# RWKV's chunk chain: both heads of a pair in one full-array matmul, and new durations in the builder's clock

## The chip, the cores and the metric

The kernel runs on one core of one Trainium2 chip. The metric is device time in microseconds (us), from the first to the last instruction of the program plus what lies around it; the median of three runs counts. PE is the matrix engine (TensorE), PEld its weight loads, DVE VectorE, ACT ScalarE, POOL GpSimd, SP the engine that issues nearly all transfers.

## What is computed

One layer of a streaming encoder, for 512 prompt tokens of one stream and 16 tokens each of 8 running streams (640 rows together), model width 1024. The reference, cut:

```python
h = _rmsnorm(x, norm_g)
proj = jnp.einsum('btd,dc->btc', h, w_in)             # 1024 x 10368
o_a = _sb_attend(q, k, v, ...)                        # 16 heads x 64, stick-breaking attention
y_a = jnp.einsum('btc,cd->btd', o_a * jax.nn.silu(z_a), w_o_a)
...
def step(S, inp):                                     # RWKV-7, 16 heads x 64, per token
    sa = jnp.einsum('bhvk,bhk->bhv', S, -kk_t)
    S = (S * w_t[:, :, None, :] + sa[..., None] * (kk_t * a_t)[:, :, None, :]
         + v_t[..., None] * k_t[:, :, None, :])
    return S, jnp.einsum('bhvk,bhk->bhv', S, r_t)
...
y = jnp.einsum('btd,de->bte', g_a * y_a + g_b * y_b, w_out)
return x + y, ...                                     # then a last rmsnorm
```

## The kernel before

**Projections.** The 81 column blocks of `w_in` (128 columns each) and the 8 blocks each of `w_o_b` and `w_o_a` are jobs of `gemm_range`. A job makes two halves of 320 or 322 rows; a half is 8 chunks of three matmuls (high by high, high by low, low by high part of fp32, tile `ps_g`), so a job is 48 matmuls. At the end `oblock` multiplies with `w_out` (tiles `ohi`, `olo`, `mgh`, `mgl`). Matmuls into `ps_g` are called projections below.

**RWKV in pairs of heads.** Heads 2p and 2p+1 lie on partitions 0-63 and 64-127. For a pair, `prep` makes from the projected rows the tiles `H`, `BK` and `AB` for ten chunks (eight of 64 prompt tokens, two with the running streams), `prep2` inverts a triangular matrix per chunk (blocks of 16 on POOL in `INV`, transposed by DVE through `STG`, then joined to 32 and 64 by small matmuls), `samp` brings in the running streams' states, and `chain` goes through the chunks in eight steps. A step first forms `RH` (matmul of `H` with `X` into `ps_b`) and the first part of the output (into `ps_c`); ACT copies `RH` out; then it forms u (`AB` with `RH`); ACT copies u into `X`; then the new state (`BKt` with `X`) and the second part of the output (`AB` with `X`); DVE writes the state to `X`, and the next step may begin. Chunks 8 and 9 (the running streams) go along in step 0, which therefore has three chunks per matmul kind. Each product stands twice, once per head, 64 columns each: `H` by `X` and `BKt` by `X` use 128 rows and 64 columns of the array, `AB` by `RH` or `X` use 64 rows and 64 columns. Every fp32 product is two instructions on PE, which is why the trace counts twice what the program has. `sstate` and `post` finish the states and the output of a pair.

**Attention in pairs of heads** (`aprep`, `attn`) starts when the last pair's `post` is through: scores (`ks` with `qh`, `ql`), two sigmoids on ACT, a running product on DVE (a scan over `kp`), a product into `bt`, transposes of `bt` on PE, a copy to `wt`, and `wt` times the values into `ps_c`. After attention the `w_o_a` jobs follow, whose operand `oAh`, `oAl` is read back through DRAM and split by POOL and DVE (`reload`).

**What sets the order.** The program is written out by a builder. `Clock` keeps an estimate of when each engine is free and each tile ready, from a table of durations in `_Eng.call`; `Driver.run` lets the streams (`prep`, `chain`, `attn` and so on, by priority) issue when their operands are ready by that estimate, and else issues a few more projections (two chunks, six matmuls, at a time) from the main program. The result is one fixed order per engine. A transpose on DVE and a scan are costed there like any other DVE operation; nothing is costed for a change of the array's shape. `calm` and the flags (`chain`, `schain`, `prep`, `amat`) gate the streams.

In `prep`, L777 waits for `chain` and `schain` of pair p-3 before `H` and `AB` are taken (three buffers each); the waits for pair p-2 stand behind the products with `H` and `BK`, ahead of `X`.

Of the kernel before, what the change touches and what calls it, by code (L numbers as in the profile page):

```python
# [26 lines left out]
F32 = mybir.dt.float32  # L27
# [8 lines left out]
D = 1024  # L36
# [52 lines left out]
class Clock:  # L89
# [5 lines left out]
    def __init__(self):  # L95
# [8 lines left out]
        self.near = dict(pe=0.25, act=0.2, dve=0.2, pool=0.15, dma=0.0)  # L104
# [99 lines left out]
class _Eng:  # L204
# [3 lines left out]
    def __getattr__(self, op):  # L208
        f = getattr(self.obj, op)

        def call(*a, **k):
# [7 lines left out]
            if e == "pe":  # L219
                w = k.get("lhsT")  # L220
                if w is None:
                    d = 0.115
                else:
                    m = _cols(w)
                    if w.dtype == F32R:
                        d = max(n / 2360.0, 0.107)
                    elif w.dtype == F32:
                        d = max(0.026 + n * 0.00087, 0.082 if m > 32 else 0.041) if m <= 64 else 0.005 + n / 600.0
                    else:
                        d = 0.06  # L230
            elif e == "act":
                d = 0.05 + n * 0.00086 + 0.1 * sum(hasattr(k.get(x), "tensor") for x in ("scale", "bias"))
# [6 lines left out]
            elif e == "dve":  # L239
                d = 0.066 + n * 0.00105  # L240
                if "scalar" in op:
                    d += 0.03 * sum(hasattr(x, "tensor") and _cols(x) == 1 for x in list(a) + list(k.values()))
                if op == "reciprocal":
                    d = 0.05 + n * 0.0064
            elif e == "pool":
                d = 0.15 + n * (0.0021 if op == "tensor_tensor" else 0.001)
                if op == "tensor_copy":
                    d = 0.2 + n * 0.0035
# [72 lines left out]
def body(tc, ins, outs, dbg=None):  # L321
# [224 lines left out]
    def start():  # L546
        x34 = pers.tile([128, 2, D], F32, tag="H", name="x34", bufs=3)
        srow = pers.tile([88, 3, 128], F32, tag="AB", name="srow", bufs=3)
# [159 lines left out]
    def prep(p):  # L708
# [68 lines left out]
        if p > 2:  # L777
            yield flag("chain", p - 3)
            yield flag("schain", p - 3)
        H = o["H"] = pers.tile([128, 2, 10, 128], F32, tag="H", name="H", bufs=3)  # L780
        AB = o["AB"] = pers.tile([128, 10, 128], F32, tag="AB", name="AB", bufs=3)
        BK = tr.tile([128, 10, 2, 64], F32, tag="BK", name="BK")
        c8 = dict(c=8)
        for h in range(2):
            rs = RS[h]
            stt(H[rs, h, 0:8, 0:64], kkn[rs, 0:512].rearrange("p (c t) -> p c t", **c8), -1.0,
                e1p[rs, :, 0:64], ALU.mult, ALU.mult)
            stt(H[rs, h, 8:10, 0:64].rearrange("p g (b t) -> p g b t", b=4),
# [34 lines left out]
        if p > 1:  # L823
            yield flag("chain", p - 2)
            yield flag("schain", p - 2)
# [931 lines left out]
```

## Time and profile before

| | |
|---|---|
| median of 3 runs | 1248.35 us (1247.88 to 1251.11) |
| profiled execution, its own time | 1252.26 us |
| its span, first to last instruction | 1250.4 us |
| mean granted clock of TensorE | 0.968 |
| busy: PE, DVE, ACT, POOL | 1157.7, 770.0, 626.3, 405.9 us |

The profile shows one execution. Matmuls overlap in the array, so the busy time of a group of them counts overlaps, and what one costs is read from the distance between starts in the timeline. "DVE X" behind an idle time names the engine and the tile that ended it. A granted clock of 1.00 is 2.4 GHz, 0.50 is 1.2 GHz.

### The profile page before, as it was taken

Reading aid. Unit: us, or ns where it says so; the run is one execution under the profiler, and the core shown is the slowest. Engines: PE = TensorE matmul, PEld = TensorE weight load, DVE = VectorE, ACT = ScalarE, POOL = GpSimd, SP = SyncE. Lnnn points to the kernel's source line nnn. Section 1 sums busy time; section 2 is a strip of 40 time slices with the busy share of each in tenths; the row PEclk is TensorE's granted clock in tenths of the full one; section 3 lists DMA queues with packets and bytes.
Section 4 is the critical chain, followed back from the end, with each engine's and each line's share of the span. In section 5 each row is a group of like instructions: output and inputs, shape, how many; then the busy total and the mean of one; then the engine's idle time right before and its main releaser. Section 6 shows DMA issues by size and latency. Waiting matters only on the chain.

```text
span 1250.4 us, 26994 instructions
## 1 busy us (share of the span) xinstructions
PE 1157.7 (93%) x10818; PEld 1033.7 (83%) x10818; DVE 770.0 (62%) x1501; ACT 626.3 (50%) x1328; POOL 405.9 (32%) x603
## 2 busy tenths in 40 slices
PE   7999899999899999999999999998898887999997
PEld 5989778888788798787787788997777776899997
DVE  5575855776856756756756742337777778654334
ACT  5637267466366474474474463534555453413223
POOL 1034341332432350351352241124444446312302
PEclk9999899999999998898999889999999997999999
DMA  5232131322212232311322322395765565246322
GB/s 193 67 107 62 54 104 47 84 88 83 72 58 77 73 85 65 88 55 58 90 58 70 84 79 80 105 255 155 204 177 143 140 177 158 88 131 185 102 100 84
DMA packets 205300, 130.79 MB, mean 105 GB/s; under 512 B 78332, under 2 KB 184696, under 8 KB 205176
## 3 DMA queue, kind: packets, MB, share of 16 engines
q1 hardware_dynamic: 204888, 129.03, 35.5%
q8 instruction: 85, 1.39, 0.5%
q14 instruction: 39, 0.32, 0.1%
q0 software_dynamic: 288, 0.05, 0.0%
HBM read 97.70 MB, written 31.35 MB: 103 GB/s over the span
## 4 chain that ended last, share of the span: by engine, by line
PE 60%; DVE 18%; ACT 11%; issue 5%; POOL 3%; DMA 2%; SPq 0%; DVEq 0%; ACTq 0%; POOLq 0%
PE ps_g L212 42%; PE ps_a L212 9%; PE ps_b L212 6%; DVE kp L212 4%; PE ps_c L212 3%; ACT STG L212 2%; DVE bt L212 2%; ACT AB L212 2%; DVE BK L212 2%; DVE H L212 1%; DVE wlo L212 1%; ACT L212 1%; DVE STG L212 1%; DVE Oa L212 1%; ACT X L212 1%
## 5 line engine op out<-in xcount | busy, mean ns | idle before, releaser
L212 PE MATMUL ps_g<-xh,whi 128*128 128x320 f32 (+1 forms) x1424 | 481.6, 338 | 0.2 <-ACT xh L212 0.2
L212 PE MATMUL ps_g<-xl,whi 128*128 128x320 f32 (+1 forms) x1424 | 448.0, 315 | 5.5 <-DVE xl L212 5.5
L212 PE MATMUL ps_g<-xh,wlo 128*128 128x320 f32 (+1 forms) x1424 | 447.5, 314 | 1.9 <-DVE wlo L212 1.9
L212 PEld LDWEIGHTS ps_g<-xh,whi 128*128 128x128 f32 x1424 | 274.1, 193 | 20.5 <-issue 5.9
L212 PEld LDWEIGHTS ps_g<-xl,whi 128*128 128x128 f32 x1424 | 274.7, 193 | 9.3 <-DVE xl L212 6.5
L212 PEld LDWEIGHTS ps_g<-xh,wlo 128*128 128x128 f32 x1424 | 274.2, 193 | 2.4 <-DVE wlo L212 2.4
L212 DVE TENSOR_TENSOR wlo<-raw,whi 128x1024 fp32r<-128x1024 f32 x97 | 123.5, 1273 | 37.5 <-ACT whi L212 36.5
L212 ACT ACTIVATE whi<-raw 128x1024 fp32r<-128x1024 f32 x97 | 102.6, 1057 | 69.7 <-PE ps_g L212 39.4
L212 POOL TENSOR_TENSOR itmp<-INV 128x28 f32<-128x28 f32 (+6 forms) x112 | 44.7, 399 | 186.5 <-DVE INV L212 178.4
L212 DVE TENSOR_TENSOR_SCAN kp<-kp,amsk 128x256 f32<-128x256 f32 (+3 forms) x80 | 77.2, 973 | 42.3 <-ACT kp L212 42.2
L212 POOL TENSOR_TENSOR bt<-bt,amsk 128x128 f32<-128x128 f32 x64 | 46.9, 738 | 140.8 <-ACT bt L212 75.6
L212 ACT ACTIVATE RH<-ps_b 128x64 f32<-128x64 f32 (+1 forms) x64 | 15.1, 236 | 119.2 <-PE ps_b L212 119.1
L212 ACT ACTIVATE kp<-ps_a 128x512 f32<-128x512 f32 (+3 forms) x72 | 33.0, 459 | 72.7 <-PE ps_a L212 47.1
L212 ACT ACTIVATE sp<-ps_g 128x320 f32<-128x320 f32 x80 | 35.0, 438 | 68.0 <-PE ps_g L212 50.9
L212 ACT ACT_TABLE_LOAD x44 | 56.5, 1283 | 20.7 <-DVE BK L212 13.5
L212 PE MATMUL ps_b<-cst,bt 128*128 128x128 f32 x192 | 34.9, 288 | 24.9 <-DVE bt L212 22.9
L212 POOL TENSOR_TENSOR ux<-X,cst 128x256 f32<-128x256 f32 x32 | 24.3, 781 | 80.2 <-PE ps_b L212 45.0
L212 DVE SCALAR_TENSOR_TENSOR X<-ps_b,wc,SW 64x64 f32<-64x64 f32 x96 | 27.0, 282 | 37.5 <-PE ps_b L212 35.8
L212 PEld LDWEIGHTS ps_b<-cst,bt 128*128 128x128 f32 x192 | 22.3, 144 | 33.1 <-issue 9.7
L212 DVE TENSOR_TENSOR bt<-bt,kp 128x511 f32<-128x511 f32 (+4 forms) x72 | 43.2, 599 | 8.8 <-POOL bt L212 2.0
L212 POOL TENSOR_TENSOR INV<-INV,itmp 128x28 f32<-128x28 f32 (+6 forms) x112 | 44.8, 400 | 8.8
L212 PE MATMUL ps_g<-olo,mgh 128*128 128x256 f32 x160 | 45.0, 281 | 0.0
(250 smaller groups left out, 2299.9 us busy)
## 6 DMA issues: line engine op xcount, KB each, us to landing
raw<-in_w_in_dram SPq DMA_DIRECT2D x81, 512.0 KB
q<-dr_q SPq DMA_DIRECT2D x32, 160.0 KB
Kr<-in_cache_sb_k_dram SPq DMA_DIRECT2D x16, 256.0 KB
Vp<-in_cache_sb_v_dram SPq DMA_DIRECT2D x16, 256.0 KB
raw<-in_w_o_b_dram SPq DMA_DIRECT2D x8, 512.0 KB
raw<-in_w_o_a_dram SPq DMA_DIRECT2D x8, 512.0 KB
oraw<-in_w_out_dram SPq DMA_DIRECT2D x4, 1024.0 KB
dr_zB<-zm SPq DMA_DIRECT2D x8, 320.0 KB
```

What stands on the lines that cost most here:

```text
L212: r = f(*a, **k)
```

## The change

`step` in `chain` multiplies both heads at once: the stationary operand holds both heads' 64 columns, the moving one both heads' 64 columns of `X`, and the result is 128x128, of which only the two diagonal blocks are used afterwards (`heads`). So that u and the output stay separate, `AB` becomes block-diagonal: two fixed tiles `ABD` of 128x10x2x128, whose off-diagonal blocks are set to zero once, by POOL, and which pairs use in turn. `H` changes its layout to put both heads side by side, and has two buffers instead of three. Therefore `prep` waits for `chain` and `schain` of pair p-2 already ahead of `H`. The output tile holds four chunks, so the eight steps are cut into groups of 2, 4 and 2 (before: 4 and 4). The second part of the change is the clock's table: other durations for nearly every kind of operation, and a cost where the array changes its shape.

```diff
-        self.near = dict(pe=0.25, act=0.2, dve=0.2, pool=0.15, dma=0.0)
+        self.near = dict(pe=0.25, act=0.15, dve=0.14, pool=0.15, dma=0.0)
+        self.mode = None
...
+                mode = "full" if r > 64 and m > 64 else (r > 32, r > 64, m > 32, m > 64)
+                if mode != self.clk.mode:
+                    d += 0.1 if self.clk.mode == "full" else 0.2
+                    self.clk.mode = mode
             elif e == "act":
-                d = 0.05 + n * 0.00086 + 0.1 * sum(hasattr(k.get(x), "tensor") for x in ("scale", "bias"))
+                d = 0.065 + n * 0.00085 + 0.1 * sum(hasattr(k.get(x), "tensor") for x in ("scale", "bias"))
+                if out.shape[0] < 64:
+                    d = 0.12 + n * 0.0021
+                elif out.shape[0] < 128:
+                    d += 0.115
...
-                d = 0.066 + n * 0.00105
...
+                d = 0.075 + n * 0.00106
+                if op == "scalar_tensor_tensor":
+                    d = 0.13 + n * 0.00112
...
+                elif op == "tensor_tensor_scan":
+                    d = 0.03 + n * 0.0025
...
+                elif op == "transpose" and len(ins[0].shape) > 2 and ins[0].ap[-1][0] > 1:
+                    d = 2.03
...
-        if p > 2:
-            yield flag("chain", p - 3)
-            yield flag("schain", p - 3)
-        H = o["H"] = pers.tile([128, 2, 10, 128], F32, tag="H", name="H", bufs=3)
-        AB = o["AB"] = pers.tile([128, 10, 128], F32, tag="AB", name="AB", bufs=3)
+        if p > 1:
+            yield flag("chain", p - 2)
+            yield flag("schain", p - 2)
+        H = o["H"] = pers.tile([128, 10, 2, 2, 64], F32, tag="H", name="H")
+        AB = o["AB"] = ABD[p % 2]
...
             for k, c in enumerate(js):
-                for h in range(2):
-                    mm(rh[RS[h], k], lhsT=H[:, h, c, 0:64], rhs=X[:, c, h, :], start=True, stop=True)
-            RH = ch.tile([128, 3, 64], F32, tag="RH", name="RH")
-            act(out=RH[:, 0:n], in_=rh[:, 0:n], func=AF.Copy)
+                mm(pv[:, k], lhsT=H[:, c, 0].rearrange("p h t -> p (h t)"), rhs=xs[c], start=True, stop=True)
+            RH = ch.tile([128, 3, 128], F32, tag="RH", name="RH")
+            act(out=RH[:, 0:n], in_=pv[:, 0:n], func=AF.Copy)
...
             for k, c in enumerate(js):
-                for h in range(2):
-                    rs = RS[h]
-                    mm(u[rs, k], lhsT=AB[rs, c, 0:64], rhs=RH[rs, k], start=True, stop=True)
+                mm(u[k], lhsT=AB[:, c, 0], rhs=RH[:, k], start=True, stop=True)
...
-            for h in range(2):
-                mm(ps[RS[h], 384:448], lhsT=BKt[:, j, h * 64:(h + 1) * 64], rhs=X[:, j, h, :],
-                   start=True, stop=True)
+            mm(pv[:, 2], lhsT=BKt[:, j, :], rhs=xs[j], start=True, stop=True)
...
-        for steps in (((0, 8, 9), (1,), (2,), (3,)), ((4,), (5,), (6,), (7,))):
+        for steps in (((0, 8, 9), (1,)), ((2,), (3,), (4,), (5,)), ((6,), (7,))):
...
+        ABD = [pers1.tile([128, 10, 2, 128], F32, name=f"AB{i}") for i in range(2)]
...
+        for t in ABD:
+            G.memset(t, 0.0)
```

How the order moves, at two places. The first is PE in the chain of the second pair. Before, the end of a step (`BKt` and `AB` with `X`) and the start of the next one (`H` with `X`), with products of the next pair's `prep` (`H` with `BK`) between them:

```order
L212 MATMUL ps_b<-X,BKt 64x64 x2
L212 MATMUL ps_c<-X,AB 64x64 x2
L212 MATMUL ps_a<-H,BK 128x128 x8
L212 MATMUL ps_b<-X,H 64x64 x2
L212 MATMUL ps_c<-X,H 64x64 x2
```

With the change, the last step of that chain, with two sums of squares of `prep` (`nrm`) between its parts:

```order
L213 MATMUL ps_b<-X,H 128x128
L213 MATMUL ps_c<-X,H 128x128
L213 MATMUL ps_a<-nrm,cst 128x320
L213 MATMUL ps_b<-RH,AB_103 128x128
L213 MATMUL ps_a<-nrm,cst 128x320
L213 MATMUL ps_b<-X,BKt 128x128
L213 MATMUL ps_c<-X,AB_103 128x128
```

Each pair of 64-column products became one of 128 columns. Counted over the stretch up to the first attention matmul, PE goes from one array shape to another 536 times before and 140 times with the change; the chain has 768 products before and 384 now.

The second place is PE in the attention of the second pair, between the transposes of the first block of `bt` and those of the next. Before:

```order
L212 MATMUL ps_g<-xh,wlo 128x320
L212 MATMUL ps_b<-cst,bt 128x128 x4
L212 MATMUL ps_a<-ks,qh 128x384
L212 MATMUL ps_a<-ks,ql 128x384
L212 MATMUL ps_b<-cst,bt 128x128 x4
L212 MATMUL ps_g<-xh,whi 128x320
```

With the change, at the same place of the same pair (the first of four such triples of projections is shown):

```order
L213 MATMUL ps_b<-cst,bt 128x128 x4
L213 MATMUL ps_a<-ks,qh 128x384
L213 MATMUL ps_a<-ks,ql 128x384
L213 MATMUL ps_g<-xh,whi 128x320
L213 MATMUL ps_g<-xl,whi 128x320
L213 MATMUL ps_g<-xh,wlo 128x320
```

Twelve projections now stand ahead of the second block's transposes. Counted from the first scores of one pair to those of the next, there are 558 projections in seven pairs before (3399 to 3957 of 5163) and 606 with the change (3573 to 4179). The last attention matmul stands behind projection 4011 before and 4239 with the change; the `w_o_a` jobs begin with projection 4300 in both.

## Rows read from the trace of the kernel before

**Rows 1.** The page: busy time, share of the span and instructions.

```profile
PE 1157.7 (93%) x10818; PEld 1033.7 (83%) x10818; DVE 770.0 (62%) x1501; ACT 626.3 (50%) x1328; POOL 405.9 (32%) x603
```

**Rows 2.** The page: chain that ended last, shares of the span by engine.

```profile
PE 60%; DVE 18%; ACT 11%; issue 5%; POOL 3%; DMA 2%; SPq 0%; DVEq 0%; ACTq 0%; POOLq 0%
```

**Rows 3.** Windows: stretch, length, busy us (instructions) per engine, PEclk, DMA, GB/s.

```profile
27.00:826.00 799.00, 754.84 (x7593) 669.17 (x7593) 498.00 (x1081) 439.67 (x920) 247.96 (x412) 0.96 0.27 78
826.00:1090.00 264.00, 231.15 (x2009) 200.67 (x2008) 184.32 (x241) 128.41 (x300) 116.22 (x137) 0.97 0.59 160
1090.00:1128.00 38.00, 38.00 (x261) 38.00 (x260) 19.78 (x25) 5.31 (x5) 5.26 (x4) 1.00 0.53 169
570.00:575.00 5.00, 5.00 (x92) 4.57 (x85) 1.74 (x5) 0.54 (x2) 0.00 (x0) 0.50 0.03 7
```

**Rows 4.** Timeline of PE, parts of a single-chunk step: start, us, operation, shapes, count.

```profile
402.27 0.31 PE L212 MATMUL ps_g<-xh,wlo 128*128 128x320 f32 x1
402.51 0.34 PE L212 MATMUL ps_b<-X,H 128*64 128x64 f32 x4
402.67 0.29 PE L212 MATMUL ps_c<-X,H 128*64 128x64 f32 x4
...
403.14 0.31 PE L212 MATMUL ps_g<-xl,whi 128*128 128x320 f32 x1
...
403.72 0.31 PE L212 MATMUL ps_g<-xh,wlo 128*128 128x320 f32 x1
403.96 0.33 PE L212 MATMUL ps_b<-RH,AB 64*64 64x64 f32 x4
...
404.48 0.31 PE L212 MATMUL ps_g<-xl,whi 128*128 128x320 f32 x1
```

**Rows 5.** Timeline of PE, the end of a later step.

```profile
410.75 0.31 PE L212 MATMUL ps_g<-xh,wlo 128*128 128x320 f32 x1
410.99 0.34 PE L212 MATMUL ps_b<-X,BKt 128*64 128x64 f32 x4
411.25 0.33 PE L212 MATMUL ps_c<-X,AB 64*64 64x64 f32 x4
...
411.77 0.31 PE L212 MATMUL ps_g<-xl,whi 128*128 128x320 f32 x1
```

**Rows 6.** Timeline of PE, three chunks of u in step 0.

```profile
397.33 0.56 PE L212 MATMUL ps_b<-RH,AB 64*64 64x64 f32 x12
...
398.08 0.31 PE L212 MATMUL ps_g<-xl,whi 128*128 128x320 f32 x1
```

**Rows 7.** Timeline of PE, two full-array fp32 products of 320 columns.

```profile
49.79 1.24 PE L212 MATMUL ps_a<-nrm,cst 128*128 128x320 f32 x4
...
51.01 0.31 PE L212 MATMUL ps_g<-xl,whi 128*128 128x322 f32 x1
```

**Rows 8.** Waits: who waited for whom, us in total, times, longest.

```profile
PE ps_b L212 <- DVE bt L212: 22.9, 28, 2.0
PE ps_b L212 <- DVE X L212: 12.3, 7, 2.6
PE ps_a L212 <- DVE STG L212: 11.5, 7, 2.6
```

**Rows 9.** Timeline of PE around a stall of the inversion.

```profile
565.66 1.05 PE L212 MATMUL ps_a<-STG,AB 16*32 16x16 f32 x64 [2.63 <-DVE STG L212]
...
568.69 0.47 PE L212 MATMUL ps_g<-xh,whi 128*128 128x322 f32 x1
568.95 0.47 PE L212 MATMUL ps_g<-xl,whi 128*128 128x322 f32 x1
```

**Rows 10.** Groups by line and form: shapes, count, busy, mean ns, idle before.

```profile
L212 DVE STREAM_TRANSPOSE STG<-INV 128x1024 f32<-128x1024 f32 x16 | 25.7, 1606 | 13.6 <-POOL INV L212 8.8 <-ACT AB L212 4.4
L212 DVE TENSOR_TENSOR_SCAN kp<-kp,amsk 128x512 f32<-128x512 f32 x16 | 24.3, 1520 | 0.0
L212 POOL TENSOR_SCALAR oAh<-rl 128x640 fp32r<-128x640 f32 x8 | 8.1, 1032 | 8.1 <-DMA rl<-dr_oA 4.6 <-PE ps_c L212 3.4
```

More of the change, by code (lines that the diff above doesn't have):

```diff
@@ L239, in call @@
             elif e == "dve":
[L240 to L244 removed]
+                d = 0.075 + n * 0.00106
+                if op == "scalar_tensor_tensor":
+                    d = 0.13 + n * 0.00112
+                elif op == "tensor_scalar":
+                    d = 0.1 + n * 0.0011 + 0.03 * sum(hasattr(x, "tensor") and _cols(x) == 1
+                                                     for x in list(a) + list(k.values()))
+                elif op == "tensor_tensor_scan":
+                    d = 0.03 + n * 0.0025
+                elif op == "reciprocal":
+                    d = 0.05 + n * 0.0064
+                elif op == "bn_stats":
+                    d = 0.126
+                elif op == "transpose" and len(ins[0].shape) > 2 and ins[0].ap[-1][0] > 1:
+                    d = 2.03
+                if out.shape[0] < 128 and any(_name(x).startswith("ps_") for x in ins if hasattr(x, "tensor")):
+                    d += 0.09
             elif e == "pool":
[L246 removed]
+                d = 0.2 + n * (0.0022 if op == "tensor_tensor" else 0.0012)
                 if op == "tensor_copy":
[L248 removed]
+                    d = 0.15 + n * 0.0035
             else:
@@ L863, in prep2 @@
         o = rw[p]
-        AB = o["AB"]
+        AB = [o["AB"][:, :, 0, 64 * (q // 2):64 * (q // 2) + 64] for q in range(4)]
+        ABt = o["AB"]
         for q in range(4):
@@ L868, in prep2 @@
             i = q % 2
[L869 removed]
+            act(out=STG[rq, :, 0:10], in_=AB[q][rq, :, 32 * i:32 * i + 32].rearrange("p u t -> p t u"), func=AF.Copy)
         yield [STG]
@@ L1049, in step @@
                 if j == 0:
-                    V.tensor_scalar_mul(out=dst, in0=ps[rs, 384:448], scalar1=wc[rs, 0:1])
+                    V.tensor_scalar_mul(out=dst, in0=heads(pv[:, 2], rs), scalar1=wc[rs, 0:1])
                 else:
-                    stt(dst, ps[rs, 384:448], wc[rs, j:j + 1], SW[rs], ALU.mult, ALU.add)
+                    stt(dst, heads(pv[:, 2], rs), wc[rs, j:j + 1], SW[rs], ALU.mult, ALU.add)
             give(ps)
             yield [X]
-        for steps in (((0, 8, 9), (1,), (2,), (3,)), ((4,), (5,), (6,), (7,))):
+        for steps in (((0, 8, 9), (1,)), ((2,), (3,), (4,), (5,)), ((6,), (7,))):
             pob = yield from take("c")
-            pov = pob[:, 0:384].rearrange("p (c v) -> p c v", c=6)
+            pov = pob.rearrange("p (c v) -> p c v", c=4)
             at0 = steps[0][0]
             for js in steps:
-                yield from step(js, [pov[:, c - at0 if c < 8 else c - 4] for c in js])
+                yield from step(js, [pov[:, c - at0 if c < 8 else c - 6] for c in js])
                 if len(js) > 1:
                     drv.spawn(sstate(p), 1)
-            act(out=Oa[:, at0:at0 + 4, :], in_=pov[:, 0:4], func=AF.Copy)
-            done = list(range(at0, at0 + 4))
+            m = len(steps)
+            for h in range(2):
+                act(out=Oa[RS[h], at0:at0 + m, :], in_=heads(pov[:, 0:m], RS[h]), func=AF.Copy)
+            done = list(range(at0, at0 + m))
             if at0 == 0:
-                act(out=Oa[:, 8:10, :], in_=pov[:, 4:6], func=AF.Copy)
+                for h in range(2):
+                    V.tensor_copy(Oa[RS[h], 8:10, :], heads(pov[:, 2:4], RS[h]))
                 done += [8, 9]
```

94 lines of the change are left out of this document (45 added, 49 removed).

## The prediction

> **What bounds the kernel now.** I read the page first: PE is busy for 1157.7 of 1250.4 us [rows 1], and 60% of the chain that ended last runs over PE, no other engine coming near [rows 2]. Then the windows by stage. From 27 to 826 us (projections with RWKV) PE is busy for 754.84 of 799 us, from 826 to 1090 (projections with attention) for 231.15 of 264, and from 1090 to 1128, where only projections are left, for all of 38 us, 261 matmuls, which is 0.1456 us each [rows 3]. So PE sets the time nearly everywhere: whatever stream has nothing ready is covered by projections, and a shorter chain is worth something only as PE time. PE can win in three ways: less work, less idle time (799 - 754.84 = 44 us in RWKV, 264 - 231.15 = 33 us in attention [rows 3]), or less time at half clock (mean granted clock 0.96 and 0.97 there [rows 3]; at 0.5 while gated, that is some 64 and 16 us at 1.2 GHz).
>
> What a burst of chain work costs is seen best in the timeline, from the projection before it to the second projection behind it, less two projections. A lone first part (`H` with `X`, four products): 403.14 - 402.27 - 0.29 = 0.58 us. A lone u: 404.48 - 403.72 - 0.29 = 0.47 [rows 4]. A lone last part: 411.77 - 410.75 - 0.29 = 0.73 [rows 5]. Together 1.78 us for a step with one chunk.
>
> How much of it is products, and how much the change of the array's shape? In the first part, the second pair of products starts 0.16 us behind the first [rows 4], 0.08 each. u with three chunks takes 398.08 - 397.33 = 0.75 us from its start [rows 6], with one 404.48 - 403.96 = 0.52 [rows 4]: four further products of 64 rows add 0.23, 0.058 each. That leaves 0.26, 0.35 and 0.73 - 0.16 - 0.12 = 0.45 us in the three bursts for seven changes of shape, about 0.15 each.
>
> The new products have a neighbour in the trace: two full-array fp32 products of 320 columns take 51.01 - 49.79 - 0.147 = 1.07 us up to the projection that follows [rows 7], 0.535 each, and nothing is lost on going from projections to them or back. For 128 columns that scales to 0.215 us.
>
> **The change part by part.**
>
> *Products.* Of 768 old ones, 448 use 128 rows (0.08) and 320 use 64 rows (0.058): 35.8 + 18.6 = 54 us. The 384 new ones take 384 x 0.215 = 83 us. That is +28 us. The array now multiplies blocks that nobody reads. For one pair of products [rows 4, 6, 7]: 2 x 0.058 = 0.116 against 0.215. The Trainium skill (TensorEngine Tiling (Array Packing), Theoretical Speedup) gives up to 2x for products with at most 64 rows or columns, which speaks against filling the array; with its factor for all products the old ones would cost 41 us and this line would be +41, an estimate.
>
> *Shape changes.* 536 before, 140 now, by the order: 396 fewer x 0.15 = -59 us. With the products, -31. As a check, the 56 steps of one chunk cost 1.78 if alone, now 5 x 0.215 = 1.08, and 56 x 0.70 = 39 us; but many bursts adjoin other small products, whose shape change remains. With 0.13 per change it is -23. I take **-30**, between -23 and -39.
>
> *The clock's table, RWKV.* The order changes where PE waits. The waits named are 11.5 us for `STG` in seven stalls and 12.3 us for `X` in seven [rows 8]. `STG` is transposed on DVE in 1.6 us on average [rows 10], which the old table put at 0.066 + 1024 x 0.00105 = 1.14; the new one has 2.03 for the strided half, so I let these 11.5 us go. `X` waits in DVE's queue behind operations that run beside POOL, whose stretching no table has: I let 4.5 of these and the smaller waits go. **-16** of 44, bounds 0 (the order fits no better) and -26.
>
> *The clock's table, attention.* PE waits 22.9 us for `bt` in 28 stalls [rows 8]. A scan of 512 takes 1.52 us [rows 10]; the old table said 0.066 + 0.54 = 0.60, the new one 1.31. The order shows the cure: 606 projections in place of 558 over seven pairs, 48 x 0.1456 = 7 us, of which twelve stand just ahead of the second block. The projections were there anyway, so the idle time they fill is gained. With the last pair and better places, **-9** of 33, bounds 0 and -18.
>
> *Half clock.* Behind the 2.63 us wait for `STG`, projections stand 0.26 us apart in place of 0.147 [rows 9], and the window from 570 to 575 shows 0.50 [rows 3]: one such stall costs some 9 us x 0.45 = 4 us more than itself. Seven at that price would be 28; the others are shorter, and I take a third, **-9**, bounds 0 and -20.
>
> *What the chain's latency does.* `RH` is twice as wide on ACT, and outputs are copied by halves of the partitions. These are latencies of a stream that waits for its turn anyway, covered by six to twelve projections; 0 for PE. If that cover is gone, PE waits inside the step, which is the bound of the first rival. Two buffers of `H`: pair p now waits for the chain of p-2 one stage earlier, ahead of `H` instead of ahead of `X`. That moves work in the order, and PE is filled with projections meanwhile: 0. Zeroing `ABD` is two POOL operations at the start, ahead of any use of `AB`: 0.
>
> *The end of attention.* This is what becomes late next. With PE time taken from RWKV and attention and projections put in, only 4300 - 4239 = 61 projections (9 us) stand between attention and the `w_o_a` jobs, before 289 (42 us). In these 9 us the last output goes through DRAM and back, and POOL copies eight parts to `oAh` at 1.03 us each [rows 10], 8.3 us in a row, DVE following with `oAl`. A job wants a part every 3 x 0.147 = 0.44 us, so the eighth is due 9 + 3 = 12 us behind attention's last matmul, and it comes at about 1 + 8.3 + 2. I take **+3**, bounds 0 and +10. SP issues the weights for the next jobs behind the store of that output; their 512 KB are due another job later.
>
> *Sum.* -30 - 16 - 9 - 9 + 3 = -61 us against the profiled execution's own 1252.3: 1191.3. That execution lay 3.9 us above the median, so **1187 us** as a median, 4.9% faster.
>
> **The rivals.**
>
> *The stalls stay.* The new table is fitted to means, while DVE beside POOL varies, and four of eight pairs now have the products for `H` and `BK` right beside the `X` copies of step 0. Then only the PE work and the short end count: -30 + 3, 1221 us. For it: 12.3 us of waits for `X` that no entry explains. Against: the `STG` and scan entries were off by 0.5 and 0.9 us, and these are corrected.
>
> *The edges stay: slower.* If the array paid the shape change also between fp32 full-array products and projections (a drain of the pipeline rather than the shape), each of the three bursts of 64 steps would keep both edges: 64 x 3 x 2 x 0.15 = 58 us of the 59 gained come back, and +28 of products remain, 1248 + 28 - 1 = 1275 us with the stalls as they are. It decides from the point where an edge costs 0.08 us. Against it stands the pair of sums of squares, which shows no edge [rows 7].
>
> *Attention ends too late.* If RWKV's longer stretch of the order (its chain ends behind projection 3309, before 3105) makes the end wait in earnest, PE stands for the whole read-back at each of the first `w_o_a` jobs, for 15 to 30 us, and the clock falls too: about 1208 us. For it: the cover fell from 42 to 9 us. Against: the parts come at nearly the pace at which they are wanted.
>
> *More than I take.* All named waits go, and the half clock with them: -39 - 26 - 18 - 20 = -103, 1145 us. It needs every bound at its best.
>
> **How the numbers follow.** Forecast 0.62 (1165 to 1210), the stalls stay 0.18, a late end 0.09, more than I take 0.06, the edges stay 0.05. About 0.3% (3.7 us) is what a measurement of this kernel can tell from no change. Faster: all but the edges and a strip of the stalls' case in which the order makes new waits of 25 us: 0.92. Same 0.03, slower 0.05. The range goes from the forecast's lower end, 1165, to just beyond the case in which the stalls stay, 1223; outside lie the edges, most of "more than I take" and some of the two other cases, about 0.2.
>
> **What the profile after should show.** In the chain, `ps_b<-X,H` with 160 instructions of 128x128 in place of 320, 0.43 us from one part's start to the next projection, and the first projection behind it at the usual distance (if it comes 0.1 later, the edges stay). PE busy in the RWKV stretch lower by some 30 us at the same number of projections. The wait of PE for `STG` near 0, that for `bt` under 15, that for `X` still near 10. Mean clock at 0.975 or more. Projections into `ps_g` from `oAh` soon behind attention, with a few us of waits for `oAl` or `oAh`. Wrong would be: PE idle in RWKV above 40 us again, idle of more than 10 us at the first `w_o_a` job, or a burst that costs as much as before.

## The result, and the profile after

The changed kernel takes 1211.51 us (1208.81 to 1212.96), the kernel before beside it 1249.73 us (1247.88 to 1251.49): a ratio of 0.9692, 95% interval 0.9665 to 0.9719. The forecast was 1187 us in a range of 1165 to 1223: the time lies in the range, 24 us above the forecast and just outside the 1165 to 1210 us that the forecast was given for itself. Of 61 us that were forecast against the profiled execution, 39.3 came (1252.26 to 1212.96). So the question is where the other 22 went, and whether the 39 came from where they were forecast.

The page of the changed kernel: busy time, share of the span (1211.2 us) and instructions.

```profile
PE 1127.9 (93%) x10050; PEld 1053.9 (87%) x10050; DVE 774.2 (64%) x1517; ACT 628.5 (52%) x1344; POOL 403.6 (33%) x605
```

PE's share is the 93% of before [rows 1]: PE works less and waits as before. Its windows, columns as in [rows 3]:

```profile
27.00:826.00 799.00, 749.35 (x6963) 710.31 (x6962) 507.85 (x1099) 447.03 (x947) 246.99 (x408) 0.97 0.27 80
826.00:1090.00 264.00, 246.78 (x2148) 219.22 (x2148) 196.90 (x266) 130.53 (x297) 114.48 (x143) 0.99 0.64 176
```

RWKV's stretch is idle for 799 - 749.35 = 50 us, more than the 44 of before; attention's for 17 in place of 33. (The stretches hold slightly other work, since the program runs ahead.) Most of the rise in RWKV is ahead of projections: they wait 5.3 us there for DVE's `wlo` and `V`, 1.9 before. By the idle times in PE's timeline, between projections, that is ahead of every product that is not one, it is 41.5 us before and 43.1 now (27 to 800 us), and 27.4 and 14.5 (800 to 1090 us); with the waits ahead of projections 43.4 and 49.1, and 32.2 and 16.5. The waits in RWKV, 27 to 826 us (us in total, times, longest), the three largest:

```profile
PE ps_b L213 <- POOL sn L213: 15.5, 6, 5.1
PE ps_b L213 <- DVE X L213: 12.2, 6, 3.9
PE ps_a L213 <- DVE BK L213: 7.1, 4, 2.9
```

`STG` (11.5 us before [rows 8]) is gone, as forecast. In its place stand `sn` and `BK`, which were 0.3 and 1.5 us before, and `X` is as it was. In attention (800 to 1090 us) the wait for `bt` fell from 22.9 us in 28 stalls [rows 8] to

```profile
PE ps_b L213 <- DVE bt L213: 14.0, 17, 1.4
```

The chain's parts, where they stand alone, cost what was forecast. PE's timeline, a lone u and a lone last part:

```profile
169.00 0.31 PE L213 MATMUL ps_g<-xh,wlo 128*128 128x320 f32 x1
169.15 0.38 PE L213 MATMUL ps_b<-RH,AB 128*128 128x128 f32 x2
169.29 0.40 PE L213 MATMUL ps_g<-xh,whi 128*128 128x320 f32 x1
169.52 0.31 PE L213 MATMUL ps_g<-xl,whi 128*128 128x320 f32 x1
...
176.14 0.30 PE L213 MATMUL ps_g<-xh,wlo 128*128 128x320 f32 x1
176.29 0.38 PE L213 MATMUL ps_b<-X,BKt 128*128 128x128 f32 x2
176.50 0.39 PE L213 MATMUL ps_c<-X,AB 128*128 128x128 f32 x2
176.65 0.39 PE L213 MATMUL ps_g<-xh,whi 128*128 128x320 f32 x1
176.88 0.31 PE L213 MATMUL ps_g<-xl,whi 128*128 128x320 f32 x1
```

From the projection before to the second one behind, less two projections: 169.52 - 169.00 - 0.29 = 0.23 us (0.47 before [rows 4]), 176.88 - 176.14 - 0.29 = 0.45 (0.73 before [rows 5]), and a first part likewise 0.45 (0.58). A step is 1.12 us in place of 1.78; the forecast had 1.08. The block products start at a projection's distance (0.15 us), so there is no edge, and the rival in which the edges stay is out.

Summed over RWKV (27 to 800 us), what lies between projections took 304.9 us before and 278.6 after; without the idle time in it, 263.4 and 235.6: 28 us less. That reads like the forecast's -30 for the products. The experiments say otherwise.

### The profile page after: what moved, and what is told of

It is laid out like the page before. It is cut to its first block, busy times and chain, and to the rows that moved or that the text cites. A ratio compares the mean times of both kernels' runs of the same rounds, so it can differ in the third digit from the quotient of the medians.

```text
span 1211.2 us, 25425 instructions
## 1 busy us (share of the span) xinstructions
PE 1127.9 (93%) x10050; PEld 1053.9 (87%) x10050; DVE 774.2 (64%) x1517; ACT 628.5 (52%) x1344; POOL 403.6 (33%) x605
## 5 line engine op out<-in xcount | busy, mean ns | idle before, releaser
L213 PE MATMUL ps_g<-xh,whi 128*128 128x320 f32 (+1 forms) x1424 | 472.7, 332 | 2.5 <-DVE V L213 2.0
L213 DVE TENSOR_TENSOR_SCAN kp<-kp,amsk 128x256 f32<-128x256 f32 (+3 forms) x80 | 74.6, 941 | 31.4 <-ACT kp L213 31.3
L213 ACT ACTIVATE RH<-ps_b 128x128 f32<-128x128 f32 (+1 forms) x64 | 19.4, 303 | 105.7 <-PE ps_b L213 105.5
L213 POOL TENSOR_TENSOR on<-on,V 128x640 f32<-128x640 f32 x8 | 13.6, 1697 | 168.2 <-ACT on L213 168.2
L213 ACT ACTIVATE kp<-ps_a 128x512 f32<-128x512 f32 (+3 forms) x72 | 33.1, 459 | 68.4 <-PE ps_a L213 43.1
L213 DVE SCALAR_TENSOR_TENSOR X<-ps_b,wc,SW 64x64 f32<-64x64 f32 x96 | 27.1, 283 | 42.8 <-PE ps_b L213 41.7
L213 DVE TENSOR_TENSOR bt<-bt,kp 128x511 f32<-128x511 f32 (+4 forms) x72 | 46.8, 650 | 8.4 <-POOL bt L213 0.9
L213 DVE TENSOR_TENSOR AB<-ps_a,cst 64x512 f32<-64x512 f32 (+1 forms) x48 | 28.6, 596 | 32.1 <-PE ps_a L213 32.0
```

The lines of the kernel that those rows point to most:

```text
L213: r = f(*a, **k)
```

## The experiments

The theory after the first look: the products gave the 28 us; the new durations gave 13 us in attention, but in RWKV they made new waits where they took old ones away. The rivals: the waits for `sn` and `BK` come with the chain's change (its products, its two buffers of `H`), or single orders scatter by chance. One suspect needs no run: with the waits for p-2 ahead of `H` and two buffers of `H` put into the kernel before, the builder writes the same order on PE, DVE, ACT and POOL with the new durations, so buffers and flags don't move anything.

All runs; idle is PE's between projections, from its timeline (27 to 800 and 800 to 1090 us; waits ahead of a projection are not in it), clock the mean granted one, cover the projections between attention and the `w_o_a` jobs by the order:

| kernel | median us | ratio (95%) | idle RWKV | idle attn | clock | cover |
|---|---|---|---|---|---|---|
| before | 1250-1252 | 1 | 41.5 | 27.4 | 0.968 | 288 |
| changed | 1211.5 | 0.9692 (0.9665-0.9719) | 43.1 | 14.5 | 0.971 | 60 |
| products_only | 1265.7 | 1.0128 (1.0095-1.0160) | 60.4 | 29.5 | 0.957 | 324 |
| table_only | 1213.5 | 0.9709 (0.9675-0.9743) | 33.6 | 12.8 | 0.974 | 222 |
| no_shape_cost | 1242.8 | 0.9936 (0.9914-0.9958) | 31.1 | 19.1 | 0.954 | 0 |
| same_order_old_shapes | 1223.8 | 0.9790 (0.9757-0.9824) | 40.6 | 13.9 | 0.970 | 60 |
| old_costs | 1215.7 | 0.9712 (0.9688-0.9736) | 37.4 | 16.1 | 0.967 | 84 |
| beside_pool | 1234.8 | 0.9870 (0.9849-0.9892) | 27.1 | 17.8 | 0.958 | 0 |
| scan_old | 1232.3 | 0.9851 (0.9832-0.9870) | 45.2 | 24.4 | 0.962 | 138 |
| table_only_beside | 1189.5 | 0.9513 (0.9491-0.9534) | 14.9 | 14.2 | 0.984 | 90 |
| old_costs_beside | 1191.7 | 0.9534 (0.9484-0.9583) | 22.6 | 15.4 | 0.984 | 36 |
| after_nudge | 1220.2 | 0.9761 (0.9720-0.9803) | 48.6 | 15.0 | 0.967 | 60 |
| beside_old_shapes | 1200.9 | 0.9593 (0.9565-0.9620) | 19.9 | 15.8 | 0.987 | 36 |
| beside_k | 1184.0 | 0.9461 (0.9435-0.9488) | 15.9 | 15.6 | 0.981 | 36 |

### The two halves of the change apart: products_only, table_only

products_only is the changed kernel with the clock's durations of before:

```diff
-        self.near = dict(pe=0.25, act=0.15, dve=0.14, pool=0.15, dma=0.0)
+        self.near = dict(pe=0.25, act=0.2, dve=0.2, pool=0.15, dma=0.0)
...
-                d = 0.075 + n * 0.00106
-                if op == "scalar_tensor_tensor":
...
+                d = 0.066 + n * 0.00105
...
```

> The changed kernel with the builder's old durations (and old allowances for following work on the same engine): block products, two buffers of H, AB zeroed once, moved waits. Theory (the chain's products give 28 us; the waits of PE for sn and for H, BK in step 0 of the chain come from the new durations, which by charging a change of shape put fewer projections ahead of that work): RWKV's idle time stays near the 41 us of before with the STG stalls of some 11 us back and sn with H, BK under 8 us together, attention's idle time near 27 us, 1222 us (1216 to 1228). Rival (two buffers of H bring the next pair's H and BK beside step 0, whatever the durations): sn with H, BK 15 us or more and the STG stalls besides, 1236 us (1230 to 1245).

table_only is the reverse: the kernel before with the new durations and nothing else.

> The kernel before with the new durations alone (old products, three buffers of H). Theory (new durations make RWKV's new stalls and gain only in attention): idle time in attention 14 to 17 us in place of 27, STG stalls under 3 us, but sn with H, BK 10 us or more, so RWKV's idle time within 5 us of 41; 1237 us (1231 to 1243). Rival (the chain's change makes the new stalls): STG stalls gone and nothing in their place, RWKV's idle time 30 or less, 1225 us (1218 to 1230).

Both theory and rival were far off. The products alone made the kernel 14 us slower (1265.7 against 1251.5); the durations alone took 38 us off, as much as the whole change. Waits of RWKV in products_only:

```profile
PE ps_b L212 <- DVE X L212: 20.9, 13, 3.4
PE ps_a L212 <- DVE STG L212: 12.7, 7, 2.2
PE ps_b L212 <- POOL sn L212: 9.8, 8, 3.5
```

and in table_only:

```profile
PE ps_b L213 <- DVE X L213: 15.0, 7, 3.8
PE ps_a L213 <- DVE nrm L213: 9.7, 3, 5.3
PE ps_b L213 <- POOL sn L213: 2.4, 2, 1.3
```

With the old durations the block products have the `STG` waits of before and 18 us more of others, for `X` (20.9 us, 12.3 before) and `sn` (9.8, 0.3 before) above all: idle in RWKV rises by 19 us and the clock falls. With the new ones and old products `sn` and `BK` (2.1 us) stay small. So the new durations do not make the waits for `sn`; nor do they cure `X`. That the durations gain in attention holds in both: 27.4 to 12.8 here, 29.5 with the old ones.

### The products alone, in one order: same_order_old_shapes

The changed kernel's order and buffers, each block product issued as the two products of before, the clock told the same (here cut to the products):

```diff
+        def two(out, lhsT, rhs, half_rows, **kw):
...
+            for h in range(2):
+                c, k = slice(h * 64, h * 64 + 64), RS[h] if half_rows else slice(0, 128)
...
+                nc.tensor.matmul(out[RS[h], oc], lhsT=lhsT[k, c], rhs=rhs[k, rc], **kw)
...
-                mm(pv[:, k], lhsT=H[:, c, 0].rearrange("p h t -> p (h t)"), rhs=xs[c], start=True, stop=True)
...
+                two(rh[:, k], H[:, c, 0].rearrange("p h t -> p (h t)"), xs[c], False, start=True, stop=True)
...
```

> The changed kernel's own order and buffers, but each product of the chain issued as two per-head products of the old shapes (64 columns, or 64 rows and 64 columns), timed for the builder as the new one. Theory (the products and shape changes are worth the 28 us of non-idle burst time that the traces differ by): 1239 us (1233 to 1245), a lone first part back at 0.55 to 0.6 us and a lone last part at 0.7 to 0.75. Rival (the gain of the shapes is smaller and the order itself gave most of it): 1222 us or less. A third (the longer bursts are hidden where PE waits anyway, since step 0 stands idle): 1228 us.

1223.8 us: between the rival's 1222 and the third case. In one and the same order the products are worth 12.3 us, not 28. The bursts say why, as they can be paired one by one: 327 in either kernel. The 70 parts with one chunk that stand alone gain 14.4 us (26 first parts 3.4, 25 u 5.95, 19 last parts 5.1), as priced. The 73 that adjoin other small products gain 7.2 us, 0.10 each. There too most changes of shape go (by the shapes in the trace from 249 to 81, in all bursts from 656 to 279), but with the products at the prediction's prices a change brings some 0.11 us in them, an estimate, against 0.14 in the bursts that stand alone, and the dearer products take most of it back. And eight mixed ones with three chunks lose 3.7. One of these, behind the inversion's products, in the changed kernel:

```profile
142.02 0.31 PE L213 MATMUL ps_g<-xh,wlo 128*128 128x320 f32 x1
142.26 0.69 PE L213 MATMUL ps_a<-AB,Y 32*32 32x32 f32 x32
142.89 0.94 PE L213 MATMUL ps_b<-X,H 128*128 128x128 f32 x6
143.66 0.83 PE L213 MATMUL ps_c<-X,H 128*128 128x128 f32 x6
144.25 0.39 PE L213 MATMUL ps_g<-xh,whi 128*128 128x320 f32 x1
144.48 0.31 PE L213 MATMUL ps_g<-xl,whi 128*128 128x320 f32 x1
```

and with the old shapes:

```profile
141.22 0.31 PE L213 MATMUL ps_g<-xh,wlo 128*128 128x320 f32 x1
141.46 0.69 PE L213 MATMUL ps_a<-AB,Y 32*32 32x32 f32 x32
142.08 0.57 PE L1038 MATMUL ps_b<-X,H 128*64 128x64 f32 x12
142.48 0.52 PE L1038 MATMUL ps_c<-X,H 128*64 128x64 f32 x12
142.93 0.42 PE L213 MATMUL ps_g<-xh,whi 128*128 128x320 f32 x1
143.19 0.31 PE L213 MATMUL ps_g<-xl,whi 128*128 128x320 f32 x1
```

2.17 us against 1.68: the six block products are 0.5 us dearer than the twelve old ones, and the change of shape at `AB,Y` (the projection before it to its start: 0.24 us in both) remains. In sum the bursts differ by 16.5 us (those without chain work and the three-chunk parts alone take 1.4 back), of which PE's waits take some back.

### What the builder is told: no_shape_cost, old_costs, scan_old

no_shape_cost:

```diff
-                    d += 0.1 if self.clk.mode == "full" else 0.2
```

> The changed kernel without the one line of the new durations that charges a change of the array's shape. Theory (that charge moves the builder's PE time ahead, so that fewer projections stand ahead of late DVE and POOL work): sn with H, BK fall from 22.5 us to under 10, 1198 us (1190 to 1205). Rival (what is missing is the slowing of DVE and POOL beside each other, and the charge has no part in it): the stalls move but their sum stays within 6 us, 1211 us (1206 to 1217).

1242.8 us; neither. RWKV's idle time did fall, to 31.1 us, but `sn` with `BK` stayed at 13.2 + 6.3. Without the charge the builder takes PE to be faster than it is and puts in more projections: the chain's end moves from projection 3309 (the prediction's count) to 3531 and attention's end to the very beginning of the `w_o_a` jobs, cover 0. There much of the time is lost, the rival "attention ends too late" of the prediction in another kernel: the window from 1090 to 1128 has PE busy for 27.84 of 38 us, at a clock of 0.61. As much again is lost from 800 to 1090 us: with the waits ahead of projections PE is idle for 31.7 us in place of 16.5, 7.3 of it in one wait of a projection for `wlo`, at a mean clock of 0.94 in place of 0.99. So the charge for a change of shape is needed, for the order of the whole.

old_costs keeps the block products and tells the clock what the two old ones cost:

```diff
+        def blk(out, lhsT, rhs, half_rows, **kw):
+            nc.tensor.matmul(out, lhsT=lhsT, rhs=rhs, **kw)
+            mode = (True, not half_rows, True, False)
+            for h in range(2):
+                d = 0.082
...
-                mm(u[k], lhsT=AB[:, c, 0], rhs=RH[:, k], start=True, stop=True)
+                blk(u[k], AB[:, c, 0], RH[:, k], True, start=True, stop=True)
...
```

> The changed kernel; only the builder's clock is told the old products' cost for each block product (two products of 64 columns with their change of shape, and RH as 64 columns), so that its order comes close to that of the kernel before with the new durations. That kernel took 1213.5 us, and the block products in an unchanged order were worth 12.3 us (1223.8 - 1211.5). Theory (the two gains add up, and 10 us of them are lost in the changed kernel only because the order that its costs give runs into the slow DVE and POOL stretch of step 0): 1201 us (1196 to 1206), waits for sn with H, BK under 10 us in place of 22.5. Rival (block products and their layout make these waits themselves): waits for sn with H, BK above 17 us, 1211 us (1207 to 1217).

1215.7 us. `sn` with `BK` fell as the theory says (4.2 + 1.9), but the time did not: `X` and `nrm` came in their place. Waits of RWKV:

```profile
PE ps_b L1030 <- DVE X L213: 18.2, 10, 3.0
PE ps_a L213 <- DVE nrm L213: 9.1, 4, 2.3
```

So the block products don't bring the waits for `sn`, and a wait that goes is replaced by another behind the same DVE queue.

scan_old takes one entry out of the changed kernel's durations:

```diff
-                elif op == "tensor_tensor_scan":
-                    d = 0.03 + n * 0.0025
```

> The changed kernel without the new durations' entry for the scan (0.60 in place of 1.31 us for 512 elements). Theory (attention's 13 us come from this entry): waits for bt back above 20 us, attention's idle time near 27 us, 1225 us (1219 to 1232). Rival (other entries, such as the copies of ACT from 64 partitions, gave it): attention's idle time under 18 us, 1212 us (1207 to 1217).

The waits of attention:

```profile
PE ps_b L213 <- DVE bt L213: 24.4, 25, 2.8
```

The theory holds: `bt` is back at 24.4 us, attention's idle time at 24.4, 10 of the 13 us that the change gained there. The time, 1232.3 us at the end of the expected range, rose by 21 us, more than this; RWKV's idle time by 2, and the mean clock fell from 0.971 to 0.962: what is missing to full clock is (1 - 0.962) x 1230 = 47 us in place of 35, which covers the rest.

### DVE and POOL beside each other: beside_pool, table_only_beside, old_costs_beside, beside_k

What the stalls for `X`, `BK`, `nrm` and `sn` have in common is read in the changed kernel's timeline (DVE, POOL, PE) of one step 0 and what follows:

```profile
329.15 5.54 POOL L213 TENSOR_TENSOR H<-R,E 64x512 f32<-64x512 f32 x4
329.81 2.12 DVE L213 SCALAR_TENSOR_TENSOR H<-kkn,E 64x512 f32<-64x512 f32 x2
...
332.59 1.81 DVE L213 TENSOR_TENSOR BK<-K,sg 64x640 f32<-64x640 f32 x1
...
336.50 1.20 DVE L213 SCALAR_TENSOR_TENSOR H<-kkn,E 64x512 f32<-64x512 f32 x2
...
338.35 1.24 DVE L213 TENSOR_TENSOR BK<-K,sg 64x640 f32<-64x640 f32 x1
...
344.60 0.69 DVE L213 TENSOR_TENSOR sn<-ps_b,S0T 128x512 f32<-128x512 f32 x1
345.37 1.04 POOL L213 TENSOR_TENSOR sn<-sn,wc 128x512 f32<-128x512 f32 x1 [5.32 <-DVE sn L213]
...
346.47 1.12 PE L213 MATMUL ps_b<-cst,sn 128*128 128x128 f32 x4 [5.09 <-POOL sn L213]
...
347.65 0.47 PE L213 MATMUL ps_g<-xl,whi 128*128 128x320 f32 x1
347.92 0.47 PE L213 MATMUL ps_g<-xh,wlo 128*128 128x320 f32 x1
```

The next pair's `H` and `BK` run on DVE beside POOL's share of `H`. The same two products for `H` take 2.12 us there and 1.20 where POOL stands idle for most of them (336.93 to 337.62). `BK` takes 1.81 us there, 1.24 beside other products of POOL's (`ux`), and 0.82 in the five of its sixteen during which POOL is idle. The chain's own small DVE work (`X`, then the sum for `sn`) queues behind, 5 us late, and the projections behind the stall start 0.27 us apart in place of 0.147: half clock (the window from 346 to 354 us has a granted clock of 0.60). The table has 0.70 us for the larger of the two products for `H` and 0.75 for `BK`, near what they take alone (0.69 and 0.82); on average over the program (mean ns, second number behind the bar) they take

```profile
L213 DVE TENSOR_TENSOR BK<-K,sg 64x640 f32<-64x640 f32 x16 | 23.8, 1484 | 0.0
L213 DVE SCALAR_TENSOR_TENSOR H<-kkn,E 64x512 f32<-64x512 f32 x16 | 21.4, 1338 | 0.2
```

and in the kernel before 1250 and 1328 ns: it was there to be read.

What the extra time is shows in single operations. The first two rows are the first of the products above; the third is the same product with POOL idle, in the kernel beside_pool below:

```profile
329.15 1.78 POOL L213 TENSOR_TENSOR H<-R,E 64x512 f32<-64x512 f32 x1
329.81 1.67 DVE L213 SCALAR_TENSOR_TENSOR H<-kkn,E 64x512 f32<-64x512 f32 x1
143.27 0.69 DVE L213 SCALAR_TENSOR_TENSOR H<-kkn,E 64x512 f32<-64x512 f32 x1
```

DVE's product ends at 331.48, 0.55 us behind the end of POOL's (330.93). So it is in nearly every case: of 594 such products of DVE (for `H`, `BK`, and `K` by `nrm`, in all fourteen traces) that take over 0.1 us more than alone, 592 end their lone time less 0.11 to 0.16 us behind the end of an operation of POOL. They are not slowed in proportion but wait for that operation, and how long depends on where POOL stands. The additions below are means of such waits.

The experiment adds to the durations:

```diff
+            nm = _name(out)
+            if out.shape[0] == 64 and nm[:1] in "HB" and not any(_name(x).startswith("ps_") for x in ins):
+                if e == "dve":
+                    d += 0.6 if n == 512 else 0.44 if n == 128 else 0.5
+                elif e == "pool":
+                    d += 0.42
```

In the changed kernel (beside_pool):

> The changed kernel with five durations more: DVE's products for H and BK on 64 partitions 0.44 to 0.6 us longer and POOL's for H 0.42 us longer, as the trace of the changed kernel has them beside each other. Theory (the waits for sn, H, BK come from this slowing, which the durations lack): these fall from 22.5 us to under 8, X from 12 to under 10, half clock less too, 1198 us (1190 to 1205); the chain ends 150 projections later, which leaves enough for attention. Rival (each new set of durations makes other stalls of the same size): RWKV's idle time within 6 us of 43, 1211 us (1205 to 1218). A third (the chain ends too late): idle time or half clock behind attention, 1215 us or more.

In the kernel before with the new durations (table_only_beside):

> The kernel before with the new durations and the five further ones for H and BK beside POOL (old products). Theory: the waits of RWKV fall from 33.6 us to 25 or less, 1206 us (1199 to 1211). Rival (each set of durations makes other stalls of the same size): 1213 us (1209 to 1220).

In old_costs (old_costs_beside):

> The block products of the changed kernel, the builder told the old products' costs for them (as in old_costs) and the five longer durations of H and BK beside POOL (as in beside_pool and table_only_beside). By the order, attention ends 36 projections (5.3 us) ahead of the w_o_a jobs, against 0 in beside_pool, 90 in table_only_beside and 60 in the changed kernel. Theory (the longer durations take the waits of step 0 away with either kind of product, the products are worth 12 us in a like order, and beside_pool lost its gain only at the end): RWKV's idle time 15 to 25 us, 1182 us (1175 to 1192). Rival (the block products bring the waits of step 0 back whatever the builder is told): RWKV's idle time 33 us or more, 1205 us (1198 to 1215). A third (the end is already too late at 36): 10 us or more of waits for oAh, oAl and wlo behind attention, 1195 us or more.

With the old products it takes 24 us off (1213.5 to 1189.5), beyond the 1206 expected; RWKV's idle time falls from 33.6 to 14.9, and its waits for `sn` and `X` are

```profile
PE ps_b L213 <- POOL sn L213: 4.7, 7, 1.3
...
PE ps_b L213 <- DVE X L213: 3.3, 5, 1.2
```

In old_costs it takes 24 us off too (1215.7 to 1191.7, idle 37.4 to 22.6). In the changed kernel it made things worse by 23 us, although RWKV's idle time fell there as well, by 16 to 27.1. The waits for `sn`, which were to fall, stayed at 16.2 us; those for `BK` went. A large part of the loss is the third case that was named, the end. Waits from 1085 us on, in beside_pool:

```profile
PE ps_g L213 <- POOL oAh L213: 5.7, 2, 4.8
PE ps_g L213 <- DVE oAl L213: 3.7, 3, 2.7
```

and its window behind attention:

```profile
1090.00:1128.00 38.00, 27.89 (x149) 23.56 (x148) 20.97 (x27) 11.78 (x21) 13.71 (x17) 0.73 0.53 179
```

With no projection left between attention and the `w_o_a` jobs (cover 0), PE stands 10 of 38 us and runs slow (0.73), some 19 us in all against the changed kernel. The rest is lost from 800 to 1090 us, where with the waits ahead of projections PE is idle for 31.1 us in place of 16.5 (a projection waits 7.3 for `wlo`, others 7.3 for `xl`), at a clock of 0.95 in place of 0.99. With 36 left, old_costs_beside loses 4.1 us in the waits for `oAh` and `oAl`; its 1191.7 us are at the upper end of what was expected, and no less than the 1189.5 with the old products.

beside_k adds one more duration to old_costs_beside, DVE's `K` by `nrm` beside POOL:

```diff
+            if e == "dve" and n == 640 and out.shape[0] == 128 and nm.startswith("K") and op == "tensor_tensor":
+                d += 0.55
```

> The kernel old_costs_beside with one duration more: DVE's K by nrm product, which takes 1.3 us on average and 1.94 us beside POOL where the builder says 0.75, is told 0.55 us longer. Theory (the waits for sn that are left, 15.2 us in eight, come from DVE's late queue in step 0, and every duration that is put right takes some away): sn 8 us or less, 1184 us (1178 to 1190). Rival (what is left scatters with the order by as much as the nudged kernel showed, 9 us, and a duration put right shows no sign of its own): 1192 us, up to 9 us to either side, sn above 10 us.

1184.0 us, as the theory has it: the wait for `sn` fell from 15.2 us in eight stalls to

```profile
PE ps_b L213 <- POOL sn L213: 5.3, 5, 1.3
```

This is the fastest kernel of the study, 5.4% below the kernel before and 2.3% below the changed one. One duration and one run: that its gain of 7.7 us is more than the scatter below is borne out by the wait that it was to remove, not by the time alone.

### The scatter of orders, and the products once more: after_nudge, beside_old_shapes

after_nudge tells the builder nothing new:

```diff
-        self.near = dict(pe=0.25, act=0.15, dve=0.14, pool=0.15, dma=0.0)
+        self.near = dict(pe=0.25, act=0.15, dve=0.16, pool=0.15, dma=0.0)
```

> The changed kernel with one allowance of the builder's clock nudged (what DVE may start ahead of its own result's time: 0.16 us in place of 0.14), which tells it nothing new; attention ends at the same projection as in the changed kernel. A measure of what the order alone may bring. If single orders scatter little: 1211 us (1208 to 1215), RWKV's idle time 40 to 46 us. If they scatter as much as the runs so far suggest: 5 us or more to either side, with the waits for sn, BK and X moved among the pairs.

1220.2 us, 8.7 slower. Waits of RWKV:

```profile
PE ps_b L213 <- POOL sn L213: 21.7, 6, 5.1
PE ps_a L213 <- DVE BK L213: 10.5, 6, 2.9
```

The same tiles, other sums. So while the durations of step 0 are wrong, which stall a pair meets hangs on chance (how far single orders scatter, one nudge does not tell), and two kernels of this builder that differ by 10 us in the order say little of their parts.

beside_old_shapes repeats the test of the products in old_costs_beside's order, by the edit of same_order_old_shapes.

> The kernel old_costs_beside with its own order and buffers, but each block product issued as the two old products (64 columns, or 64 rows and 64 columns); the same pair of kernels as the changed one and same_order_old_shapes, in an order with few waits. Theory (the shapes are worth what the bursts show: 86 parts stand alone there, 32 x 0.23 + 31 x 0.13 + 23 x 0.28 = 17.9 us, the others gain 0.1 us each, the three-chunk first part behind the AB, Y products loses 0.5): 1209 us (1204 to 1214). Rival (in an order with few waits the chain's own latency decides, and the shapes matter no more than the 2 us between old_costs_beside and table_only_beside): 1194 us (1189 to 1199).

1200.9 us (1199.8 to 1201.5) against 1191.7 (1190.5 to 1193.9): 9.2 us, between the two expectations (7 us by the two ratios, each taken beside its own runs of the kernel before). The bursts differ by 11.2 us: 87 parts alone give 16.7, the 58 mixed ones 2.2 (0.04 each in place of the 0.10 expected), mixed ones with three chunks lose 4.3, and 3.6 are lost in bursts without chain work. So the shapes are worth 9 to 12 us in either order. The waits for `sn` are 15.3 us with the old shapes and 15.2 with the new, in eight stalls each: they come with the order, not with the block products.

## Why the prediction came out as it did

By its terms, against the runs:

| term | forecast | shown |
|---|---|---|
| products and shape changes | -30 (-23 to -39) | -12.3 and -9.2, in two orders |
| idle in RWKV | -16 (0 to -26) | +1.6 (+5.7 with the waits ahead of projections) |
| idle in attention | -9 (0 to -18) | -13 (-16 likewise) |
| half clock | -9 (0 to -20) | about -6 |
| end of attention | +3 (0 to +10) | about +1 |

The values shown add to -29 of the 39 us. The other 10 came with the new order and had no term: same_order_old_shapes lies 26 us below the kernel before, some 17 of it in idle time and half clock, the rest in PE's work. That the time lies in the range is in part luck. Two terms came some 18 us short each, and 14 us that the forecast lacked here and in attention made up for a good part. Of the signs of being wrong that it named, one came (PE idle in RWKV above 40 us again), and the mean clock, 0.971, stayed below its 0.975.

*Products and shape changes.* The step that failed is the price in "536 before, 140 now, by the order: 396 fewer x 0.15 = -59". The count held: in one order 377 changes go. The price came from parts that stand alone, where it is right: some 0.14 a change, and 1.12 us a step against 1.08 forecast. But only 70 of the parts with one chunk stand alone; beside other small products a change brought some 0.11, most of which the dearer products took back, and eight bursts with three chunks lost (whether there the changes gave less than 0.15 or the products cost more than 0.215, the bursts do not tell). I named this ("many bursts adjoin other small products") and let it lower the price by 0.02 in the bound, where the term should have been built from bursts: so many alone by 0.13, 0.23 and 0.28, so many mixed by 0.1, and eight of three chunks against. In the bursts the term came to -16.5, and in time, with what PE's waits took back, to -12.3; even the bound of -23 was about twice that. The factor that the prediction drew from the Trainium skill (TensorEngine Tiling (Array Packing), Theoretical Speedup) would have made the term +41 - 59 = -18, an estimate, nearer the runs; but not for its own reason, as the lone parts show the products at the price I took.

*The 28 us that the traces show* in RWKV's bursts seem to confirm the term, and don't: the part that the products don't explain came with the order, which the pair in one order separates. In the changed order PE goes through 327 stretches of small products in place of 344, and loses some 19 us in them to half clock in place of 23. What each of the two is worth was not tried.

*Idle in RWKV.* The `STG` stalls went, as forecast, and new ones came of the same sum, which is the rival "the stalls stay" with its 1221 us: in RWKV that is what happened. Its reason was named right (DVE beside POOL varies, and no entry has it), and its chance of 0.18 was too low. The step that failed is that of a named wait I took away its us, as if PE met no other behind it. The runs show the opposite five times: with the DVE queue of step 0 costed too short, `sn`, `BK`, `X` and `nrm` take each other's place (products_only, table_only, old_costs, scan_old, after_nudge), and with it costed near the trace RWKV's idle time falls by 15 to 19 us in all three kernels (11 to 16 with the waits ahead of projections). Even then `sn` kept 15 to 16 us in two of the three.

*Idle in attention* came from the scan's entry, as argued: 10 of the 13 us go with it.

*Half clock.* By the mean clock, (1 - 0.968) x 1250 = 40 us were lost to it before and (1 - 0.971) x 1211 = 35 after. Summed over windows of 10 us, PE ran some 75 us at half clock before and 63 after, of which half is lost: 6 us. In RWKV alone it is 58 and 56, for it follows the stalls, and these stayed.

*The end.* 0.55 us of waiting for `oAl` and 0.7 for `wlo` with 60 projections of cover: less than forecast. The rival "attention ends too late" did not occur here, but stands one step further: the two kernels with cover 0 lost more there (some 23 and 19 us from 1090 to 1128) than they gained in RWKV.

What stays open: why the block products with the old durations are 14 us slower, when in a given order they are 9 to 12 us faster. Over the whole span PE is idle for 102 us in place of 84 and loses 54 to half clock in place of 40, while the rest of its time is some 20 us shorter: the products seem to gain there too, and stalls take more than that. The waits named (`X` in 13 stalls in place of 7) show where, and the nudge shows that an order may cost 9 us by chance; which of the layout's steps shifts it was not tried.

## What to carry to other kernels

A gain per burst holds for bursts that stand alone: count the neighbours before multiplying. A wait that is removed is a gain only if nothing queues behind it; where an order is built from estimated durations, compare these with the trace operation by operation, above all where two engines run side by side, since five corrected durations brought 24 us in two kernels here (and cost 23 in a third, whose attention then ended too late), and the new products 9 to 12. And where an order can change, test a part with the order held fixed: in free orders one nudge was worth 9 us, and two traces side by side credited the products with what the order had given.

## What the runs showed of the hardware that was not expected

DVE's products for `H`, `BK` and `K` wait for operations of POOL's that run beside them: the larger product for `H` takes 0.69 us with POOL idle and 1.62 on average (up to 2.08, 142 cases in the fourteen traces) where POOL works throughout, and 592 of 594 such long products end at a fixed distance, their lone time less 0.11 to 0.16 us, behind the end of an operation of POOL. POOL's own `H` product of 64x512 takes 1753 ns on average where the builder has 1.33 us. Six fp32 products of the full array are dearer than twelve that use half its columns: the burst above takes 2.17 against 1.68 us, while two lone ones gain by the edges alone.
